# The first two tiles' modulation and the sums of the first squares on TensorE, and a longer stated landing time of loads in a list schedule

## The chip, the cores and the metric

The program runs on one core of a Trainium2 chip. The metric is the device time of one execution in microseconds (us). The kernel is written in Bass: each engine (PE is TensorE, DVE is VectorE, ACT is ScalarE, POOL is GpSimd, SP is SyncE, which issues all the DMAs here) works through its own queue in the order in which the program issued the instructions, and semaphores keep the engines in step.

## What is computed

A trunk of two layers over x (1024 tokens, 1024 channels, float32). Each sub-layer starts with an RMS norm and an adaLN modulation from a conditioning vector c. Layer 0 mixes tokens by a gated MLP, layer 1 by a gated linear recurrence; each is followed by a convolutional FFN. Cut to what matters:

```python
cond = jax.nn.silu(c)
for i in range(DEPTH):
    mod = (cond @ ada_w[i] + ada_b[i])[:, None, :]
    sh1, sc1, g1, sh2, sc2, g2 = jnp.split(mod, 6, axis=-1)
    h = rms_norm(x, norm_g[i, 0]) * (1.0 + sc1) + sh1
    y = (spatial_gating_mixer if i % 2 == 0 else hgrn2_mixer)(h, ...)
    x = x + g1 * y
    h = rms_norm(x, norm_g[i, 1]) * (1.0 + sc2) + sh2
    x = x + g2 * conv_ffn(h, ...)
return rms_norm(x, final_g)
```

The first thing that the first matrix product (h @ w_in of the mixer) needs is h: the sum of squares of x over the channels, and for each channel sc1 and sh1, two dot products of cond with columns of ada_w.

## The kernel before

x is kept transposed: eight tiles d = 0..7 of 128 channels by 1024 tokens, in two halves of 512 tokens (LO and HI). Each large product is made of float32 operands that are split into a rounded part (hi, by ACT, L500 for weights, L487 for h) and the rest (lo, by DVE or POOL, L503 and L488), and takes three matrix products for one (`mm3`, L280): hi x hi, hi x lo, lo x hi. Strassen-like combinations save products in the later stages.

**What sets the order.** All work is entered in a plan (`pl.op`) with the engine, a stated duration, what it reads and writes, and a priority. `Plan.schedule` is a list schedule over the stated durations: it takes again and again the operation that can start earliest, by priority where several can. A result of a DMA counts as there LOAD = 2.0 us after the stated end of its transfer (`lag`); loads that `p_ada` enters count ADA_LAG = 1.5 us later still. The schedule is run twice; in the second run the priorities are the latest start times that follow from the PE order of the first. The instructions are then issued in that order, so a stated time moves instructions in every queue, but no instruction waits for a stated time.

**The start.** The program's first work is this:
- PE multiplies a tile of ones by itself as a filler (`warm`, L968), 14 times, later 10 and 8 times; nothing reads the result.
- SP issues the loads of x (LO) in five transfers (L996), the row of c behind the third of them (L994), then rows of ada_w (two 512 KB transfers a tile, one for the scale and one for the shift), parameters and weights of the values (wv), in the order A0 W W A1 W A2 W ... W W W W of the loop over items.
- PE broadcasts the row of c to all partitions by two products with ones (L1004); ACT and DVE make silu of it (L1006, L1007).
- ACT squares the eight tiles of x (L454, the last by L1016), DVE adds the first seven squares into one tile (L459), and PE sums the last square and that tile over the partitions: eight products with a column of ones (L1020).
- DVE makes the inverse root of the four columns (L314 to L324) and spreads it into a diagonal (L368), PE broadcasts that by a product with ones (L373).
- For each tile d, `first_values` makes the two dot products of cond with rows of ada_w on DVE (L288, a multiply over 128 x 1024 with its sum), adds the bias (L296), makes the factor (L300), and multiplies x by it and the inverse root (L1042); ACT and DVE make the hi and lo part of h from it (L487, L488). For tile 0 one of the dot products is entered ahead (`p_dot`).
- `first_mms` enters the products of tile d with the split weights: eight PSUM banks, three products each. For tile 0 the eight hi x hi products come first by themselves.

After these come the rest of the values, the spatial gating (`GmUp`), the output product (`block_out`, read out by L442 of `p_evac`), the FFN (`Ffn`), the recurrence (`HgUp`, `Unit`), and the second FFN. The dot products for the later modulations are entered through all these stages by `p_ada`, one transfer and one DVE instruction each.

## Time and profile before

| | before |
|---|---|
| median of 3 runs | 2400.89 us |
| lowest and highest | 2396.86 and 2404.48 us |
| the profiled execution | 2402.39 us |
| its span, from the first to the last instruction | 2400.6 us |
| mean granted clock of PE in it | 0.994 |
| PE busy | 2370.1 us (99% of the span) |
| DVE busy | 2063.9 us (86%) |
| ACT busy | 1288.8 us (54%) |
| POOL busy | 449.9 us (19%) |

The profile is of one execution. Times are counted from its first instruction. A float32 product stands in it as two records, one that came from rounded operands as one. PEclk is the share of the full TensorE clock (2.4 GHz) that was granted; 0.50 is the lower of its two levels, 1.2 GHz. A busy PE is not a PE at its peak.

### The profile page before, as it was taken

To read this page: it belongs to the slowest core of one execution; us is meant where nothing else is said; L and a number is where in the kernel's file an instruction comes from. 1 tells how busy PE (TensorE), PEld (TensorE's weight loads), DVE (VectorE), ACT (ScalarE), POOL (GpSimd) and SP (SyncE) were. 2 spreads that over 40 slices of the span, in tenths; PEclk is the share of its full clock that TensorE was granted. 3 is DMA by queue.
4 is the path that set the end of the run, shared out by engine and by line. 5 is a ranking of instruction groups with operands and counts; after the bars stand their busy time and mean duration, and the time that the engine had idled before them with its cause. 6 is when DMAs were issued, how large, how long until landed. Compare 5 with 4: busy or idle time off the path is not lost.

```text
span 2400.6 us, 32858 instructions
## 1 busy us (share of the span) xinstructions
PE 2370.1 (99%) x11358; PEld 1976.7 (82%) x11358; DVE 2063.9 (86%) x3322; ACT 1288.8 (54%) x2301; POOL 449.9 (19%) x312
## 2 busy tenths in 40 slices
PE   9999999999999999999999999999999999999998
PEld 7888887788888888888788888888888888887886
DVE  8899988988989889998988788887689988898756
ACT  4546664455555555445566666665255555544444
POOL 0222110322222221012301111111122222220121
PEclk8999999999999999999999999999999999999999
DMA  9667769720333324865301111225313333338332
GB/s 338 194 217 255 238 205 308 258 81 27 123 96 121 113 92 143 296 218 180 122 15 52 45 45 45 71 62 157 105 42 110 104 117 108 107 123 285 95 104 97
DMA packets 154827, 330.91 MB, mean 138 GB/s; under 512 B 15522, under 2 KB 34338, under 8 KB 154660
## 3 DMA queue, kind: packets, MB, share of 16 engines
q1 hardware_dynamic: 154660, 328.81, 41.8%
q8 instruction: 89, 1.46, 0.3%
q14 instruction: 78, 0.64, 0.1%
HBM read 253.77 MB, written 74.98 MB: 137 GB/s over the span
## 4 chain that ended last, share of the span: by engine, by line
PE 93%; DVE 2%; DMA 2%; issue 1%; ACT 1%; POOL 0%; SPq 0%; POOLq 0%; ACTq 0%; DVEq 0%
PE pb L280 85%; PE pb L1626 4%; PE pb L1346 1%; PE pb L1691 1%; PE pb L1711 1%; DMA h<-act 0%; PE pb L1713 0%; DVE w L503 0%; DMA xT<-vd 0%; PE pb L373 0%; DVE h L503 0%; PE pb L1684 0%; PE pb L1734 0%; DMA h<-gact 0%; DMA w<-in_down 0%
## 5 line engine op out<-in xcount | busy, mean ns | idle before, releaser
L280 PE MATMUL pb<-h,w 128*128 128x512 f32 (+1 forms) x4470 | 1038.5, 388 | 8.5 <-ACT h L500 2.9
L280 PEld LDWEIGHTS pb<-h,w 128*128 128x128 f32 x4470 | 832.5, 188 | 184.8 <-ACT h L500 4.2
L280 PE MATMUL pb<-n,w 128*128 128x512 f32 x3312 | 790.1, 391 | 1.8 <-ACT wk L735 1.0
L280 PEld LDWEIGHTS pb<-n,w 128*128 128x128 f32 x3312 | 617.6, 188 | 130.7 <-ACT wk L735 1.5
L503 POOL TENSOR_TENSOR w<-w,w 128x512 fp32r<-128x512 f32 x170 | 260.5, 1537 | 952.2 <-ACT w L500 913.9
L500 ACT ACTIVATE w<-w 128x512 fp32r<-128x512 f32 x405 | 249.8, 627 | 265.4 <-PE pb L280 162.0
L893 DVE SCALAR_TENSOR_TENSOR raw<-wk,prm,raw 128x1024 f32<-128x1024 f32 x168 | 266.3, 1594 | 7.4 <-ACT raw L889 6.3
L503 DVE TENSOR_TENSOR w<-w,w 128x512 fp32r<-128x512 f32 x235 | 169.8, 728 | 32.6 <-ACT w L500 31.7
L500 ACT ACTIVATE w<-n 128x512 fp32r<-128x512 f32 x136 | 85.8, 631 | 163.8 <-PE pb L280 151.6
L735 ACT ACTIVATE wk<-pb 128x512 f32<-128x512 f32 x160 | 94.7, 593 | 139.9 <-PE pb L280 117.7
L280 PE MATMUL pb<-w,n 128*128 128x512 f32 x612 | 144.5, 397 | 3.6 <-DVE n L488 3.6
L738 DVE TENSOR_TENSOR wk<-pb,wk 128x512 f32<-128x512 f32 x160 | 108.3, 686 | 45.5 <-PE pb L280 40.8
L280 PEld LDWEIGHTS pb<-w,n 128*128 128x128 f32 x612 | 116.5, 191 | 29.8 <-DVE n L488 4.5
L503 POOL TENSOR_TENSOR w<-raw,w 128x512 fp32r<-128x512 f32 x55 | 78.5, 1440 | 328.6 <-ACT w L500 216.9
L503 DVE TENSOR_TENSOR w<-n,w 128x512 fp32r<-128x512 f32 x136 | 101.1, 746 | 44.5 <-ACT w L500 44.1
L500 ACT ACTIVATE h<-h 128x512 fp32r<-128x512 f32 x198 | 121.8, 618 | 25.1 <-DMA h<-gact 12.8
L889 ACT ACTIVATE raw<-wk,prm 128x1024 f32<-128x1024 f32 x84 | 103.6, 1240 | 32.8 <-DVE raw L510 12.9
L280 PE MATMUL pb<-w,h 128*128 128x512 f32 x480 | 116.9, 396 | 0.0
L503 DVE TENSOR_TENSOR h<-h,h 128x512 fp32r<-128x512 f32 x150 | 110.2, 739 | 6.9 <-ACT h L500 6.9
L503 POOL TENSOR_TENSOR h<-h,h 128x512 fp32r<-128x512 f32 x48 | 67.9, 1414 | 197.9 <-ACT h L500 186.2
L280 PEld LDWEIGHTS pb<-w,h 128*128 128x128 f32 x480 | 88.1, 188 | 17.4
L442 DVE SCALAR_TENSOR_TENSOR xT<-pb,mod,xT 128x512 f32<-128x512 f32 (+1 forms) x108 | 74.4, 727 | 24.5 <-PE pb L280 24.2
(278 smaller groups left out, 2927.9 us busy)
## 6 DMA issues: line engine op xcount, KB each, us to landing
w<-in_up SPq DMA_DIRECT2D x88, 512.0 KB, 3.7
act<-raw SPq DMA_DIRECT2D x154, 256.0 KB, 2.2
h<-act SPq DMA_DIRECT2D x124, 256.0 KB, 2.8
h<-in_ada SPq DMA_DIRECT2D x45, 512.0 KB, 4.7
wk<-in_ada SPq DMA_DIRECT2D x33, 512.0 KB, 4.6
n<-in_down SPq DMA_DIRECT2D x64, 256.0 KB, 5.4
gact<-xT SPq DMA_DIRECT2D x56, 256.0 KB, 3.8
h<-gact SPq DMA_DIRECT2D x56, 256.0 KB, 3.9
```

What stands on the lines that cost most here:

```text
L280: PE.matmul(ps, L[i // 2], R[i % 2], start=first and i == 0 and not more, stop=last and i == 2, skip_group_check=more)
L442: V.scalar_tensor_tensor(out=xT[:, d, hs], in0=ps.f, scalar=gate(d), in1=xT[:, d, hs], op0=ALU.mult, op1=ALU.add)
L500: pl.op("S", 0.2 + 0.43 * w, lambda: S.activation(hi.r, src.f, AF.Copy), r=(src,), w=(hi,), pr=pr)
L503: lambda: e.tensor_tensor(out=lo.r, in0=src.f, in1=hi.f, op=ALU.subtract), *preds,
L735: pl.op("S", 0.6, lambda: S.activation(c.f, ps.f, AF.Copy), r=(ps,), w=(c,), pr=p(i) - 10)
L738: pl.op("V", 0.69, lambda: V.tensor_tensor(out=c.f, in0=ps.f, in1=c.f, op=ALU.add), r=(ps, c), w=(c,), pr=p(i) - 8)
L889: pl.op("S", 1.22, lambda: S.activation(y.f, wk[:, o + PADW:o + PADW + T], AF.Identity, bias=pc("conv_b", l * NUP + b), scale=cw(2)), r=(c ...
L893: pl.op("V", 1.26, lambda w=w: V.scalar_tensor_tensor(out=y.f, in0=wk[:, o + w:o + w + T], scalar=cw(w), in1=y.f, op0=ALU.mult, op1=ALU.ad ...
L1346: PE.matmul(ps.f[:, i * P:(i + 1) * P], v.f[:, i * P:(i + 1) * P], wsT[:, j, :], start=True, stop=True)
L1626: PE.matmul(ps_()[0:m, c, :], K.f[:, c * P:c * P + m], q, start=True, stop=True)
L1691: PE.matmul(b2.f[:, cs(c)], kT.f[:, cs(c)], vc(c), start=True, stop=True)
L1711: PE.matmul(b3.f[:, cs(c)], sc.f[:, cs(c)], vc(c), start=True, stop=s_ is None)
```

## The change

Three things change.
- **Sums of squares.** ACT squares all eight tiles into four buffers in turn (L1028 of the changed kernel), and PE sums each square by four products with a column of ones as it comes (L1032): 32 products that add up in one bank. DVE adds no squares.
- **Modulation of tiles 0 and 1.** c is loaded a second time as columns (`cc`, 128 x 8), ACT and DVE make silu of it, and for tiles 0 and 1 PE makes the two dot products each with the weights laid out in another way in memory (`adaf`): eight products with one column each (`pe_dots`, L1051). `first_values` reads the sums from PSUM. Tiles 2 to 7 keep DVE's dot products.
- **The stated times.** LOAD is 3.0 and ADA_LAG 0.5. Fillers are 7, 4 and 4; in the plan a second group of them has 3 rather than 10, all into another bank.

The two loads of c now stand ahead of x in SP's queue. The split of the first weights no longer has the first tile ahead of it in the plan.

```diff
-ADA_LAG = 1.5
+ADA_LAG = 0.5
+NPE = 2
-    LOAD = 2.0
+    LOAD = 3.0
...
-    def ada_group(l, w, d=0, n=KT, nw=1):
+    def ada_group(l, w, d=0, n=KT, nw=1, ps=None):
...
-        V.tensor_tensor(out=v, in0=v, in1=cols(pc("ada_b", l * 48, 48)), op=ALU.add)
+        src = v if ps is None else ps.rearrange("p (w d) -> p w d", d=n)
+        V.tensor_tensor(out=v, in0=src, in1=cols(pc("ada_b", l * 48, 48)), op=ALU.add)
...
-    pl.op("D", 0.1, lambda: nc.sync.dma_start(condr[0:1, :], a["crow"]), w=(rv(2),), pr=SB - 31)
+    def load_cond():
+        nc.sync.dma_start(cc, a["ccol"])
+        nc.sync.dma_start(condr[0:1, :], a["crow"])
+    pl.op("D", 0.2, load_cond, w=(ccrg, rv(2)), pr=SB - 32)
+    pl.op("S", 0.25, lambda: S.activation(csig, cc, AF.Sigmoid), w=(ccrg,), pr=SB - 32)
+    pl.op("V", 0.17, lambda: V.tensor_tensor(out=csl, in0=cc, in1=csig, op=ALU.mult), w=(ccrg,), pr=SB - 32)
...
-    warm(10, 0.3, SB - 29)
+    warm(3, 0.3, SB - 29)
...
-    for d in range(KT - 1):
-        p_sum(pl, nm0, d, accv, sqs3, SB - 3)
-    pl.op("S", 0.63, lambda: S.activation(sq.f, xT[:, KT - 1, LO], AF.Square), r=(xrg(KT - 1, LO),), w=(sq,), pr=SB - 3)
-    for i, x in enumerate((sq, accv)):
+    for d in range(KT):
+        q = sqs.next()
+        pl.op("S", 0.6, lambda d=d, q=q: S.activation(q.f, xT[:, d, LO], AF.Square), r=(xrg(d, LO),), w=(q,), pr=SB - 25 + d)
...
+                PE.matmul(ps0.f[:, c:c + 1], q.f[:, c * P:(c + 1) * P], ones[:, 0:1], start=d == 0 and c == 0,
+                          stop=d == KT - 1, skip_group_check=True)
+        last = pl.op("PE", 0.7, fn, r=(q, onesrg), w=(ps0,), pr=SB - 25 + d)
+    warm(4, 0.22, SB - 40, last)
...
+    def pe_dots(d, raws):
+
+        for m, raw in raws:
+            def fn(raw=raw, col=m // KT):
+                for k in range(KT):
+                    PE.matmul(psd[d].f[:, col:col + 1], raw.f[:, k * P:k * P + P], csl[:, k:k + 1], start=k == 0, stop=k == KT - 1)
+            pl.op("PE", 1.2, fn, r=(raw, ccrg), w=(psd[d],), pr=SB - 2.5 + d)
...
-            ada_group(0, 0, d, 1, 2)
+            ada_group(0, 0, d, 1, 2, psd[d].f[:, 0:2] if d < NPE else None)
...
-            p_load(pl, x, a["ada"][0, m], pr)
-        if d == 0:
-            p_dot(*raws.pop(0), SB, after)
+            p_load(pl, x, a["adaf"][m // KT, d] if d < NPE else a["ada"][0, m], pr)
+        if d < NPE:
+            pe_dots(d, raws)
+            raws = []
```

PE's queue from the program's first instruction to the first L280 product, before (pb6 holds the sums, h6 and the like are weight buffers):

```order
L968 MATMUL pb7_82<-ones_69 128x128 x14
L1004 MATMUL pb4_79<-raw2_67,ones_69 128x512
L1004 MATMUL pb5_80<-raw2_67,ones_69 128x512
L1020 MATMUL pb6_81<-ones_69,wk_68 128x1 x8
L968 MATMUL pb7_82<-ones_69 128x128 x10
L373 MATMUL pb6_81<-wk_68,ones_69 128x512
L968 MATMUL pb7_82<-ones_69 128x128 x8
L280 MATMUL pb0_75<-w4_177,n000_203 128x512
```

The same stretch of PE's queue in the changed kernel, whose lines are one to thirty higher (L281 is L280 of before, L375 is L373, L970 is L968):

```order
L970 MATMUL pb3_78<-ones_69 128x128 x7
L1015 MATMUL pb4_79<-raw2_67,ones_69 128x512
L1015 MATMUL pb5_80<-raw2_67,ones_69 128x512
L1032 MATMUL pb6_81<-ones_69,wk_68 128x1 x32
L970 MATMUL pb3_78<-ones_69 128x128 x4
L1051 MATMUL pb7_82<-cc_74,h6_114 128x1 x8
L1051 MATMUL pb7_82<-cc_74,h7_129 128x1 x8
L375 MATMUL pb6_81<-wk_68,ones_69 128x512
L970 MATMUL pb3_78<-ones_69 128x128 x4
L1051 MATMUL pb5_80<-cc_74,h11_141 128x1 x8
L1051 MATMUL pb5_80<-cc_74,h0_189 128x1 x8
L281 MATMUL pb0_75<-w4_211,n000_225 128x512
```

The sums have grown from 8 to 32 products, tile 0's dot products stand between them and the broadcast, tile 1's between the broadcast and the first L281 product.

DVE's queue from the diagonal of the inverse root to the low part of tile 0, before:

```order
L368 TENSOR_TENSOR wk<-prm,small 128x512
L288 SCALAR_TENSOR_TENSOR h_119,mod<-h_119,raw_67 128x1024
L288 SCALAR_TENSOR_TENSOR h_128,mod<-h_128,raw_67 128x1024
L296 TENSOR_TENSOR mod<-mod,prm 128x2
L300 SCALAR_TENSOR_TENSOR amul<-mod,prm 128x1
L1042 SCALAR_TENSOR_TENSOR xT<-xT,amul,pb_81 128x512
L503 TENSOR_TENSOR w_200<-h_135,w_167 128x1024
L503 TENSOR_TENSOR w_205<-h_143,w_177 128x1024
L288 SCALAR_TENSOR_TENSOR h_163,mod<-h_163,raw_67 128x1024
L288 SCALAR_TENSOR_TENSOR h_173,mod<-h_173,raw_67 128x1024
L296 TENSOR_TENSOR mod<-mod,prm 128x2
```

The same stretch of DVE's queue in the changed kernel (L370, L1062, L505 and L490 are L368, L1042, L503 and L488 of before):

```order
L370 TENSOR_TENSOR wk<-prm,small 128x512
L298 TENSOR_TENSOR mod<-pb_82,prm 128x2
L302 SCALAR_TENSOR_TENSOR amul<-mod,prm 128x1
L1062 SCALAR_TENSOR_TENSOR xT<-xT,amul,pb_81 128x512
L505 TENSOR_TENSOR w_223<-h_158,w_201 128x1024
L505 TENSOR_TENSOR w_238<-h_165,w_211 128x1024
L298 TENSOR_TENSOR mod<-pb_80,prm 128x2
L302 SCALAR_TENSOR_TENSOR amul<-mod,prm 128x1
L1062 SCALAR_TENSOR_TENSOR xT<-xT,amul,h_236 128x512
L490 SCALAR_TENSOR_TENSOR n_241<-xT,mod,n_225 128x512
L505 TENSOR_TENSOR w_260<-h_199,w_243 128x1024
L490 SCALAR_TENSOR_TENSOR n_267<-xT,mod,n_256 128x512
```

The four dot products are gone from it, and the two groups wait for PE's sums in PSUM (pb_82 and pb_80) instead.

DVE's queue in the output product of layer 0, between the read-out of banks 6 and 7 (pb_81, pb_82) and that of bank 0 (pb_75), before:

```order
L442 SCALAR_TENSOR_TENSOR xT<-pb_82,mod,xT 128x512
L503 TENSOR_TENSOR w_2897<-raw_65,w_2897 128x512
L503 TENSOR_TENSOR h_3019<-h_2967,h_3019 128x512
L503 TENSOR_TENSOR w_2937<-raw_65,w_2937 128x512
L503 TENSOR_TENSOR h_3035<-h_2962,h_3035 128x512
L288 SCALAR_TENSOR_TENSOR h_3209,mod<-h_3209,raw_67 128x1024
L503 TENSOR_TENSOR w_2826<-n_2842,w_2826 128x512
L296 TENSOR_TENSOR mod<-mod,prm 128x8
L300 SCALAR_TENSOR_TENSOR amul<-mod,prm 128x8
L288 SCALAR_TENSOR_TENSOR raw_66,mod<-raw_66,raw_67 128x1024
L503 TENSOR_TENSOR w_2855<-n_2848,w_2855 128x512
```

The same place of DVE's queue in the changed kernel (L444 is L442 of before, L289 is L288):

```order
L289 SCALAR_TENSOR_TENSOR h_3234,mod<-h_3234,raw_67 128x1024
L505 TENSOR_TENSOR w_2934<-raw_65,w_2934 128x512
L505 TENSOR_TENSOR h_3076<-h_3004,h_3076 128x512
L444 SCALAR_TENSOR_TENSOR xT<-pb_81,mod,xT 128x512
L444 SCALAR_TENSOR_TENSOR xT<-pb_82,mod,xT 128x512
L505 TENSOR_TENSOR w_2974<-raw_65,w_2974 128x512
L505 TENSOR_TENSOR h_3080<-h_2999,h_3080 128x512
L298 TENSOR_TENSOR mod<-mod,prm 128x8
L302 SCALAR_TENSOR_TENSOR amul<-mod,prm 128x8
L505 TENSOR_TENSOR w_2861<-n_2878,w_2861 128x512
L289 SCALAR_TENSOR_TENSOR h_3234,mod<-h_3234,raw_67 128x1024
L505 TENSOR_TENSOR w_2891<-n_2884,w_2891 128x512
```

One dot product and two splits that stood behind the read-out of banks 6 and 7 stand ahead of it now.

## Rows read from the trace of the kernel before

**Rows 1.** The page, busy us (share of the span) xinstructions of each engine.

```profile
PE 2370.1 (99%) x11358; PEld 1976.7 (82%) x11358; DVE 2063.9 (86%) x3322; ACT 1288.8 (54%) x2301; POOL 449.9 (19%) x312
```

**Rows 2.** Windows, the dense stretch: us, busy by engine, PEclk, DMA share, GB/s.

```profile
26.55:2388.30 2361.75, 2348.01 (x11262) 1958.91 (x11262) 2041.08 (x3268) 1274.56 (x2283) 446.19 (x303) 1.00 0.42 135
```

**Rows 3.** Timeline, PE's first 50 us: start, us, line, tiles, records, idle before.

```profile
1.05 5.29 PE L968 MATMUL pb<-ones 128*128 128x128 f32 x28 [1.05 <-DVE ones L992]
7.28 2.64 PE L1004 MATMUL pb<-raw,ones 1*128 1x512 f32 x4 [0.94 <-DMA raw<-in_crow]
9.86 3.57 PE L1020 MATMUL pb<-ones,wk 128*128 128x1 f32 x16
13.29 4.61 PE L968 MATMUL pb<-ones 128*128 128x128 f32 x20
17.70 1.53 PE L373 MATMUL pb<-wk,ones 128*128 128x512 f32 x2
19.06 1.95 PE L968 MATMUL pb<-ones 128*128 128x128 f32 x16
20.82 2.10 PE L280 MATMUL pb<-w,n 128*128 128x512 f32 x8
26.55 23.63 PE L280 MATMUL pb<-w,n 128*128 128x512 f32 x91 [3.62 <-DVE n L488]
```

**Rows 4.** Timeline, DVE's first 28 us.

```profile
13.47 0.16 DVE L314 TENSOR_SCALAR small<-pb 128x4 f32<-128x4 f32 x1 [0.50 <-PE pb L1020]
...
15.45 0.69 DVE L368 TENSOR_TENSOR wk<-prm,small 128x512 f32<-128x512 f32 x1
...
19.27 0.75 DVE L1042 SCALAR_TENSOR_TENSOR xT<-xT,amul,pb 128x512 f32<-128x512 f32 x1 [0.45 <-PE pb L373]
19.93 2.35 DVE L503 TENSOR_TENSOR w<-h,w 128x1024 fp32r<-128x1024 f32 x2
22.20 1.22 DVE L288 SCALAR_TENSOR_TENSOR h<-h,raw 128x1024 f32<-128x1024 f32 x1
...
25.75 0.75 DVE L488 SCALAR_TENSOR_TENSOR n<-xT,mod,n 128x512 fp32r<-128x512 f32 x1
```

**Rows 5.** Windows, stretches of one clock level in the first 60 us.

```profile
5.05:8.47 3.42, 2.48 (x14) 1.76 (x14) 2.16 (x4) 2.95 (x6) 0.00 (x0) 1.00 1.05 401
8.47:13.20 4.73, 4.73 (x18) 3.34 (x16) 3.28 (x5) 3.79 (x7) 0.00 (x0) 0.50 1.03 406
13.20:18.70 5.50, 5.50 (x24) 4.98 (x24) 4.82 (x17) 2.49 (x3) 0.00 (x0) 0.50 1.02 408
...
25.53:32.36 6.83, 5.81 (x14) 4.56 (x15) 6.73 (x12) 3.10 (x4) 0.00 (x0) 0.50 1.01 340
...
40.00:60.00 20.00, 20.00 (x90) 16.53 (x90) 19.32 (x36) 9.10 (x13) 0.00 (x0) 1.00 0.85 307
```

**Rows 6.** Groups by form, PE, near 82 us: busy us, mean ns, idle.

```profile
L363 PE MATMUL pb<-ones,wk 128*128 128x1 f32 x8 | 0.9, 239 | 0.0
```

**Rows 7.** Timeline, SP's queue, the first issues.

```profile
0.74 1.47 SPq L996 DMA_DIRECT2D xT<-in_x  x3
2.24 0.37 SPq L994 DMA_DIRECT2D raw<-in_crow  x1
```

**Rows 8.** Timeline, ACT's squares and sigmoids in the first 14 us.

```profile
4.78 1.15 ACT L454 ACTIVATE wk<-xT 128x512 f32<-128x512 f32 x2 [2.77 <-DMA xT<-in_x]
...
9.12 0.61 ACT L454 ACTIVATE wk<-xT 128x512 f32<-128x512 f32 x1
...
11.05 1.08 ACT L1006 ACTIVATE xT<-pb 128x512 f32<-128x512 f32 x2
```

**Rows 9.** Waits of PE: us in total, times, longest us.

```profile
PE pb L280 <- DVE xT L442: 2.6, 1, 2.6
```

**Rows 10.** Timeline, DVE and PE at the read-out near 449 us.

```profile
446.99 1.22 DVE L288 SCALAR_TENSOR_TENSOR raw<-raw,raw 128x1024 f32<-128x1024 f32 x1
...
449.34 2.72 DVE L442 SCALAR_TENSOR_TENSOR xT<-pb,mod,xT 128x512 f32<-128x512 f32 x4
...
450.23 2.09 PE L280 MATMUL pb<-h,w 128*128 128x512 f32 x8 [2.62 <-DVE xT L442]
```

34 lines of the change are left out of this document (18 added, 16 removed).

## Prediction

> **What bounds the kernel now.** I read the page's busy times first: TensorE (PE) is busy in 99% of the span, the next engine in 86% [rows 1]. Then the busy time of one long stretch: from 26.55 to 2388.30 us PE is busy 2348.01 of 2361.75 us, so only 13.74 us of idling are spread over all that lies between the start and the tail [rows 2]. Two things follow. Whatever reaches the end must pass through PE, and a delay of PE before 26.55 has almost nothing behind it that could swallow it. So the question is when the dense stream of L280 products begins; the timeline of PE shows that at 26.55 us only eight of them have been done, at 20.82 [rows 3].
>
> What sets 26.55 now: the sums of squares end on PE at 13.43 (9.86 + 3.57); VectorE (DVE) makes the ten small steps and the diagonal, 13.47 to 16.14; PE broadcasts, 17.70 to 19.23; DVE forms tile 0 at 19.27, makes two splits, two dot products for tile 1 from 22.20 on, tile 1's group and the low part at 25.75 to 26.50 [rows 3, 4]. So the last part is DVE's, the first is PE's.
>
> A third view is needed: the granted clock. It is 0.50, the lower level of 1.2 GHz, from 8.47 to 18.70 and again from 25.53 to 32.36, else 1.00 [rows 5]. The first of these stretches matters most. It began while PE was on the condition row's products (L1004), and it stayed low although PE was busy without a gap: 4.73 of 4.73 us up to 13.20, nearly all of it on L1004 and on the one-column products L1020, then 5.50 of 5.50 on fillers (L968) and the broadcast. The clock rose only at the end of the fillers.
>
> **What the change does to PE's queue.** The order has, before the first L280 product: 7 fillers, the two condition products, 32 one-column sums, 4 fillers, 16 one-column dot products of tile 0, the broadcast, 4 fillers, 16 of tile 1. Before it was 14, 2, 8, 10, broadcast, 8. One-column products go from 8 to 64, fillers from 32 to 15.
>
> Price of a one-column product at the low clock: L1020's eight products are sixteen records in 3.57 us; without the last one's own 0.35 that is 0.215 a record, 0.43 a product. At the high clock L363's eight records of the same shape took 0.9, with a last one of about 0.24: 0.09 to 0.11 a record, 0.22 a product at the most [rows 3, 6]. So the price doubles with the low clock. The planner states 0.7 for four and 1.2 for eight, less than either.
>
> The Trainium skill ("TensorE: Matmul & The Clock Gate", Part 2, LDWEIGHTS) prices a weight load by its columns at a fixed 1.2 per ns, 107 ns for 128, whatever the array's clock. By that figure 64 records of sums would be an estimated 6.8 us at any clock; the trace disagrees at the low level with its 215 ns, and the measured price is used.
>
> I take the low clock for the whole start, because the nearest rows are L1020's own, and reason on the other case below. Then, in the time of the profiled execution:
>
> 1. Seven fillers at 0.46 (ten took 4.61) from 1.05: to 4.3. The condition row is now issued second, ahead of the x tiles, not behind three of them, so it should be there by then; its two products took 2.64, partly at the high clock [rows 3, 7]: to between 6.9 and 7.8, I take 7.2.
> 2. The x loads are issued two places later, some 0.9 us (three issues took 1.47), so the first square, at 4.78 before, comes at about 5.7 and is done at 6.3 [rows 7, 8]. A square is 0.58, its four sums 1.7, so PE sets the pace. 32 x 0.43 = 13.8: to 21.0, where it was 13.43.
> 3. Four fillers 1.8 (22.8), tile 0's sixteen dot products 6.9 (29.7), broadcast 1.53 to 1.9 (31.4). DVE's chain of 2.7 lies beside it and is ready at 23.7. Tile 0 is formed at 31.5; before at 19.27.
> 4. Four fillers (33.2), tile 1's sixteen 6.9 (40.1), eight L280 products at 0.43: to 43.5. Beside them DVE makes the two splits (2.35, after tile 0) and, after 40.1, the group (two small steps, about 0.2 each as in the chain), tile 1 and the low part (0.75 each), with gaps 2.1: ready at 42.2, before PE asks at 43.5. The saved dot products of tile 1, 2.3 us of DVE on the path before, therefore give nothing, nor do the seven additions of squares and the two of tile 0.
> 5. The clock. After 26.55 it stayed low for 5.81 us of dense products. I take the same from 40.1, to 45.9: 13.5 products at 0.43 are then done, where at 32.36 it had been 13.5 and the eight earlier ones. Delay: 45.9 - 32.36 = 13.5, and eight products at 0.22 (90 in 20.00 at the high clock [rows 5]) 1.8: 15.3 us.
>
> ScalarE's squares need the buffers that the sums free, and its second sigmoid stands behind five squares; both are done near 15, six us before anything asks. The dot products hold their four weight buffers until 40, and SyncE's queue waits there in order, with the loads of tiles 3 and 4 behind. DVE comes to tile 3 only after the low part at 42.2, a split (1.2), another low part (0.7), tile 2's two dot products (2.4), its group and forming (1.1) and a split (1.2), so near 49; loads issued between 27 and 30, when tile 0's buffers come free, have 19 us to land. Cost nothing; without that cover each us that a load is late would be a us of delay.
>
> **The stated landing time.** 2.0 becomes 3.0 for all loads, and the ada loads of the later stages keep 3.5 (2.0 + 1.5, now 3.0 + 0.5). No work is added; the order on all engines shifts. Bounds: the gain is at most the 13.74 us of rows 2; the loss has no row, and I bound it by as much again. The one large wait shows what a shift does: PE waits 2.62 us for the results read out by L442 at 447.6 to 450.2, and DVE reaches L442 at 449.34 behind two dot products of 1.22 and splits [rows 9, 10]. In the new order one of these dot products and two splits stand ahead of the read-out of pb6 and pb7 instead: 2.6 us less here, and as much more for those. I take 0, with 4 us to either side, as the largest single wait is 2.6.
>
> **Sum.** 2402.39 (the profiled execution, span 2400.6) + 15.3 + 0 = 2417.7. The median of the runs is 1.5 lower: **2416**.
>
> **The rivals.** (a) *The clock rises.* If it were high over the sums, one-column products would cost 0.22. The last square would end near 11.5 (the last took 9.12 to 9.73; 0.9 for the two issues and two sigmoids of 0.54 come before it now), the sums at 12.4, fillers 0.9, dot products 3.6 (16.9), broadcast (18.2), fillers 1.0, dot products 3.6 (22.8), eight products 1.8 (24.6). DVE's low part for tile 0 would be ready at 24.9. Dense from 24.9, not 26.55, gains 1.7, and the low stretch of 5.81 at half speed is gone, 2.9 more: 4.6 faster, at the median 2396. This is the case on the other side: not slower. It decides if the clock is high by about 8 us and stays there. For it speaks that 28 records of fillers were followed by a stretch at 1.00; against it that the clock fell during L1004 and did not come back in the 3.57 us of L1020. The Trainium skill (the same page, Part 1) says that sustained activity releases the throttle and advises keeping the engine busy; taken by itself that rule gives this rival; the trace agrees where the fillers and the dense products ran, not where L1020 did.
>
> (b) *The clock is high in part*, say from the dot products on: they save 32 x 0.21 = 6.7, fillers and broadcast 1.5, the low stretch of the dense stream 2.9, of the 15.3: 4 slower, 2405.
>
> (c) *The new order gives back more than it may*: most of the 13.74 vanishes beside the delay of the main case, 15.3 - 11: 2405. That needs all dozen waits, of several kinds, to improve together.
>
> (d) *The order costs*: new waits of 8 us beside the delay: 2424.
>
> **How the numbers follow.** Main case 0.72 (2411 to 2421: 4 us for the order, 1 for the condition row and the end of the low stretch), (a) 0.10, (b) 0.09, (c) 0.05, (d) 0.04. The range 2404 to 2422 takes in the main case, (b) and (c). A measurement of this kernel tells 0.3%, 7.2 us, from no change: slower is above 2408. The main case is slower but for a tail of some 0.02, and with (d) that makes 0.74; same is 0.22, from that tail, (b), (c) and 0.06 of (a); faster 0.04, the part of (a) in which the order gives 3 us as well.
>
> **What would show it.** In the new trace the 64 records of L1032 should stand 0.21 apart, end near 21, and the clock should read 0.50 from before them until some us after the first L281 product; tile 0 (L1062) near 31, the first L281 near 40. If the records stand 0.11 apart, rival (a) holds and step 2 fails. If PE waits between L1032's groups, squares or x loads set the pace and the step on the loads is wrong. If DVE's low part comes after the eight products, step 4 is. If the start is as worked out but the total is not, the order in the rest is the cause, and PE's idle time after the start, 13.74 now, will show it.

## The result and the profile after

| | before | after |
|---|---|---|
| median | 2402.01 us (6 runs) | 2414.31 us (6 runs) |
| lowest and highest | 2396.86 and 2404.48 us | 2411.70 and 2420.87 us |
| the profiled execution | 2402.39 us | 2420.87 us |
| its span | 2400.6 us | 2418.8 us |

The changed kernel takes 1.0057 times as long, with an interval of 1.0046 to 1.0069: 12.3 us more by the medians, 13.7 by the ratio (11 to 17 by its interval), nearly twice the 0.3% that a measurement of this kernel can tell from no change. The forecast was 2416. The profiled execution of the changed kernel is the longest of its six; that matters where its trace is summed up.

The page of the changed kernel, busy us (share of the span) xinstructions, the line that answers to [rows 1]:

```profile
PE 2393.9 (99%) x11436; PEld 1999.0 (83%) x11436; DVE 2047.3 (85%) x3309; ACT 1289.8 (53%) x2301; POOL 454.2 (19%) x312
```

PE is 23.8 us busier, and DVE 16.6 us less. The timeline of PE tells where (start, us, line, tiles, records, idle before), against [rows 3]; here L970 is the filler, L1015 the condition row's products, L1032 the sums, L1051 the dot products, L375 the broadcast and L281 the dense products:

```profile
1.05 3.36 PE L970 MATMUL pb<-ones 128*128 128x128 f32 x14 [1.05 <-DVE ones L994]
4.34 3.78 PE L1015 MATMUL pb<-raw,ones 1*128 1x512 f32 x4
8.04 13.81 PE L1032 MATMUL pb<-ones,wk 128*128 128x1 f32 x64
21.72 2.05 PE L970 MATMUL pb<-ones 128*128 128x128 f32 x8
23.57 6.83 PE L1051 MATMUL pb<-cc,h 128*128 128x1 f32 x32
30.25 2.05 PE L375 MATMUL pb<-wk,ones 128*128 128x512 f32 x2
32.10 1.91 PE L970 MATMUL pb<-ones 128*128 128x128 f32 x8
33.81 6.83 PE L1051 MATMUL pb<-cc,h 128*128 128x1 f32 x32
40.49 21.75 PE L281 MATMUL pb<-w,n 128*128 128x512 f32 x83
```

Before the first dense product PE has no gap behind 1.05 us, so the start is all PE's own work. The two loops of one-column products are the two long rows: 13.81 us for 64 records of sums (0.216 each) and twice 6.83 us for 32 of dot products (0.213 each).

DVE's timeline, against [rows 4] (L316 is the first small step, L370 the diagonal, L298 the group, L1062 the forming of a tile, L505 splits, L490 the low part):

```profile
21.89 0.16 DVE L316 TENSOR_SCALAR small<-pb 128x4 f32<-128x4 f32 x1 [6.65 <-PE pb L1032]
...
23.87 0.69 DVE L370 TENSOR_TENSOR wk<-prm,small 128x512 f32<-128x512 f32 x1
...
30.43 0.16 DVE L298 TENSOR_TENSOR mod<-pb,prm 128x2 f32<-128x2 f32 x1 [5.86 <-PE pb L1051]
...
32.34 0.75 DVE L1062 SCALAR_TENSOR_TENSOR xT<-xT,amul,pb 128x512 f32<-128x512 f32 x1 [1.56 <-PE pb L375]
33.01 2.35 DVE L505 TENSOR_TENSOR w<-h,w 128x1024 fp32r<-128x1024 f32 x2
...
41.81 0.74 DVE L490 SCALAR_TENSOR_TENSOR n<-xT,mod,n 128x512 fp32r<-128x512 f32 x1
```

Before, DVE was the last on this path; now it waits 6.65 and 5.86 us for PE. The work that was taken off DVE had become its waiting time.

The windows of the changed kernel (us, PE busy, PEld, DVE, ACT, POOL, granted clock, DMA share, GB/s), first of the end of the start, then of the whole dense stretch, then of two short stretches far behind:

```profile
40.50:46.20 5.70, 5.70 (x15) 4.44 (x16) 5.38 (x9) 2.62 (x3) 0.00 (x0) 1.00 0.64 205
46.20:60.00 13.80, 13.80 (x62) 11.44 (x61) 13.49 (x25) 5.08 (x6) 0.00 (x0) 1.00 0.87 275
...
50.00:2406.60 2356.60, 2343.72 (x11242) 1955.23 (x11240) 2025.59 (x3258) 1274.34 (x2279) 450.49 (x303) 1.00 0.41 134
...
988.30:991.60 3.30, 3.30 (x10) 2.55 (x9) 3.21 (x5) 1.14 (x3) 0.00 (x0) 0.50 0.97 313
...
2193.20:2196.50 3.30, 3.30 (x9) 2.61 (x8) 3.30 (x4) 0.07 (x1) 0.00 (x0) 0.50 1.02 363
```

The clock column has a trap. This trace holds no entry of the clock ahead of a rise at 46.18 us, so the first row prints 1.00. But its 15 dense records in 5.70 us are 0.38 apart, against 62 in 13.80 us, 0.22, in the next row: up to 46.18 us the lower level of 1.2 GHz was granted. The Trainium skill ("TensorE: Matmul & The Clock Gate", Part 1) warns that clock events in a trace can be unreliable; here the spacing of the records decides, and a run below shows nearly the same start with its clock entered as 0.50.

The third row is [rows 2] again: PE idles 12.88 us between the start and the tail (2356.60 less 2343.72), where it was 13.74. The last two rows show something that the profile of before did not have: behind waits of PE of 2.21 us at 984.67 and of 0.36 and 1.16 us at 2190.38 the clock was at its lower level from 988.26 to 991.68 us and from 2193.17 to 2196.58. At half speed each of these costs 1.7 us, an estimate: half of its 3.41 us.

The sum of the profiled executions. The clock is up at 46.18 instead of 32.36, and eight dense products fewer are done by then: 13.8 + 1.8 = 15.6 us. Idle time behind it: 12.88 - 13.74 = -0.9. The two falls of the clock: +3.4. Together 18.1, and the spans differ by 18.2. The medians differ by 12.3 only, because the profiled execution is 6.6 us above its median, and that of before 0.4 above.

### The profile page after: what moved, and what is told of

Its sections match the earlier page's. It is cut to its first block, busy times and chain, and to the rows that moved or that the text cites. A ratio compares the mean times of both kernels' runs of the same rounds, so it can differ in the third digit from the quotient of the medians.

```text
span 2418.8 us, 33051 instructions
## 1 busy us (share of the span) xinstructions
PE 2393.9 (99%) x11436; PEld 1999.0 (83%) x11436; DVE 2047.3 (85%) x3309; ACT 1289.8 (53%) x2301; POOL 454.2 (19%) x312
## 4 chain that ended last, share of the span: by engine, by line
PE 92%; DVE 4%; issue 2%; DMA 1%; ACT 1%; POOL 0%; SPq 0%; POOLq 0%; DVEq 0%; ACTq 0%
PE pb L281 82%; PE pb L1647 4%; PE pb L1367 1%; PE pb L1032 1%; PE pb L1732 1%; PE pb L1712 1%; DVE raw L895 1%; PE pb L1051 1%; DVE w L505 1%; PE pb L1734 0%; DVE h L505 0%; PE pb L375 0%; ACT xT L1344 0%; PE pb L1705 0%; PE pb L1554 0%
## 5 line engine op out<-in xcount | busy, mean ns | idle before, releaser
L281 PE MATMUL pb<-h,w 128*128 128x512 f32 (+1 forms) x4470 | 1042.3, 390 | 9.7 <-DVE h L505 3.9
L281 PEld LDWEIGHTS pb<-h,w 128*128 128x128 f32 x4470 | 834.3, 188 | 187.1 <-DVE h L505 5.4
L281 PE MATMUL pb<-n,w 128*128 128x512 f32 x3312 | 790.3, 392 | 1.4 <-ACT wk L737 1.2
L281 PEld LDWEIGHTS pb<-n,w 128*128 128x128 f32 x3312 | 617.4, 188 | 130.8 <-ACT wk L737 2.1
L505 POOL TENSOR_TENSOR w<-w,w 128x512 fp32r<-128x512 f32 x170 | 259.6, 1532 | 885.3 <-ACT w L502 803.6
L895 DVE SCALAR_TENSOR_TENSOR raw<-wk,prm,raw 128x1024 f32<-128x1024 f32 x168 | 255.6, 1536 | 13.0 <-ACT raw L891 12.1
L505 DVE TENSOR_TENSOR w<-w,w 128x512 fp32r<-128x512 f32 x235 | 168.6, 726 | 29.7 <-ACT w L502 27.5
L505 POOL TENSOR_TENSOR w<-raw,w 128x512 fp32r<-128x512 f32 x55 | 84.0, 1539 | 336.4 <-ACT w L502 273.6
L281 PE MATMUL pb<-w,n 128*128 128x512 f32 x612 | 143.7, 396 | 0.0
L281 PEld LDWEIGHTS pb<-w,n 128*128 128x128 f32 x612 | 116.7, 191 | 25.4 <-issue 1.0
L505 DVE TENSOR_TENSOR w<-n,w 128x512 fp32r<-128x512 f32 x136 | 99.4, 732 | 44.7 <-ACT w L502 43.7
L281 PE MATMUL pb<-w,h 128*128 128x512 f32 x480 | 117.0, 396 | 0.0
L505 DVE TENSOR_TENSOR h<-h,h 128x512 fp32r<-128x512 f32 x150 | 111.1, 745 | 4.5 <-ACT h L502 4.5
L505 POOL TENSOR_TENSOR h<-h,h 128x512 fp32r<-128x512 f32 x48 | 68.5, 1427 | 206.1 <-ACT h L502 194.9
L444 DVE SCALAR_TENSOR_TENSOR xT<-pb,mod,xT 128x512 f32<-128x512 f32 (+1 forms) x108 | 74.4, 728 | 34.1 <-PE pb L281 33.9
L281 PEld LDWEIGHTS pb<-w,h 128*128 128x128 f32 x480 | 88.1, 188 | 17.8
```

The costliest lines, as they stand in the source:

```text
L281: PE.matmul(ps, L[i // 2], R[i % 2], start=first and i == 0 and not more, stop=last and i == 2, skip_group_check=more)
L444: V.scalar_tensor_tensor(out=xT[:, d, hs], in0=ps.f, scalar=gate(d), in1=xT[:, d, hs], op0=ALU.mult, op1=ALU.add)
L505: lambda: e.tensor_tensor(out=lo.r, in0=src.f, in1=hi.f, op=ALU.subtract), *preds,
L895: pl.op("V", 1.26, lambda w=w: V.scalar_tensor_tensor(out=y.f, in0=wk[:, o + w:o + w + T], scalar=cw(w), in1=y.f, op0=ALU.mult, op1=ALU.ad ...
```

## The experiments

Each was timed beside the kernel before, on the same chip as that. To compare starts, I give each kernel's *dense start*: the time at which the stream of dense products would have begun, without a gap and at the high clock. For the kernel before: first dense product behind the wait at 26.55, low clock to 32.36, so half of 5.8 lost, and eight products of 0.22 done ahead: 26.55 + 2.9 - 1.8 = 27.7. For the changed kernel: 40.49, low to 46.18: 43.3.

| kernel | dense start, us | PE idle from 50 us to the tail | later falls of the clock in its profile | median, us | ratio to before |
|---|---|---|---|---|---|
| before | 27.7 | 13.74 | 0 | 2401.6 to 2402.3 | 1 |
| the change | 43.3 | 12.88 | 2 | 2414.31 | 1.0057 [1.0046, 1.0069] |
| its start alone | 42.8 | 17.56 | 0 | 2419.13 | 1.0067 [1.0055, 1.0079] |
| its stated times alone | 26.9 | 12.82 | 1 | 2399.79 | 0.9991 [0.9982, 1.0000] |
| sums and dots 128 columns wide | 27.0 | 11.70 | 2 | 2402.22 | 0.9997 [0.9988, 1.0005] |
| only the sums wide | 31.0 | 11.72 | 1 | 2407.34 | 1.0023 [1.0014, 1.0032] |
| only the sums on PE | 29.2 | 12.89 | 1 | 2405.86 | 1.0020 [1.0011, 1.0029] |
| only the dots on PE | 30.5 | 12.05 | 2 | 2405.49 | 1.0013 [1.0005, 1.0022] |
| the change with ten fillers | 43.0 | 11.23 | 2 | 2418.78 | 1.0072 [1.0059, 1.0086] |
| both wide, start rearranged | 24.9 | 10.86 | 1 | 2403.25 | 1.0003 [0.9994, 1.0012] |
| the same, times 2.0 and 1.5 | 25.5 | 11.71 | 0 | 2401.59 | 0.9998 [0.9987, 1.0009] |
| the same, times 3.0 and 1.5 | 26.2 | 11.02 | 0 | 2399.26 | 0.9985 [0.9975, 0.9994] |
| the same, times 2.5 and 0.5 | 26.8 | 14.39 | 1 | 2409.50 | 1.0022 [1.0009, 1.0034] |

The columns account for the profiles: the span of each, less its dense start, its idle time and 1.7 us for each fall, leaves 2357.8 to 2360.1 us in all thirteen. What a median differs by beside that is the spread between executions.

**The start and the stated times.** The start of the changed kernel under the old stated times:

```diff
-ADA_LAG = 0.5
+ADA_LAG = 1.5
-    LOAD = 3.0
+    LOAD = 2.0
```

> The changed start with the old stated times (2.0 and 1.5). Theory (the start costs its own delay, the order of the rest next to nothing): first L281 product near 40.5 us as in the changed kernel, low clock until about 46, and about 15.6 us slower than before, near 2417. Rival (the new order gives part of the delay back, since the changed kernel's median is only 12.3 above): the same start, and 18 us or more slower, near 2420.

Measured: 2419.13 us (2415.30 to 2422.38), 17.2 above before, between the theory's 15.6 and the rival's 18. Its first dense product in the timeline, the whole dense stretch in its windows, and its wait for the read-out in the output product of layer 0, which was [rows 9] before:

```profile
40.49 9.70 PE L281 MATMUL pb<-w,n 128*128 128x512 f32 x32
```

```profile
50.00:2408.30 2358.30, 2340.74 (x11239) 1952.28 (x11237) 2029.86 (x3258) 1271.94 (x2279) 449.58 (x303) 1.00 0.41 134
```

```profile
PE pb L281 <- DVE xT L444: 2.9, 1, 2.9
```

In the changed kernel the same row of the waits reads:

```profile
PE pb L281 <- DVE xT L444: 1.4, 1, 1.4
```

The start carries the loss. What it also does is change the idle time far behind it: 17.56 us, 3.8 more than before, under the same stated times. The new stated times take 4.7 of that away again; the wait at the read-out gives 1.5 of them. In the medians that is 4.8 us, but the two ratios' intervals overlap, so the size is not certain from the times alone.

The other half, the stated times alone in the kernel before:

```diff
-ADA_LAG = 1.5
+ADA_LAG = 0.5
-    LOAD = 2.0
+    LOAD = 3.0
```

> The kernel before with the new stated times (3.0 and 0.5) alone. Theory: start as before (first of the dense stream near 26.5), total within 2 us of before, 2400 to 2404, as waits of PE after the start change by about 1 us in sum. Rival (the order gives back some 3 us or more): 2399 or less. Other rival (the order adds waits that make the clock fall in the middle): 2404 to 2407.

Measured: 2399.79 us (2395.53 to 2404.70), 2.2 less than before, at the edge of what can be told apart and just below the theory's range. Its dense stream in the timeline, then windows of it:

```profile
25.70 24.60 PE L280 MATMUL pb<-w,n 128*128 128x512 f32 x95 [3.62 <-DVE n L488]
```

```profile
31.60:2387.70 2356.10, 2343.28 (x11250) 1955.41 (x11248) 2027.65 (x3259) 1274.28 (x2281) 447.05 (x303) 1.00 0.41 135
```

It idles 12.82 us instead of 13.74. So the stated times are worth one to five us in either start, never the loss.

**Is it the number of products, or the clock they run at?** Same products, same order, same count, but the moving operand of each sum and dot product is 128 equal columns instead of one. Nothing is taken away, and the results are read from one of the columns.

```diff
-  PE.matmul(ps0.f[:, c:c + 1], q.f[:, c * P:(c + 1) * P], ones[:, 0:1], ...
+  PE.matmul(ps0.f[:, c * P:(c + 1) * P], q.f[:, c * P:(c + 1) * P], ones, ...
...
-  PE.matmul(psd[d].f[:, col:col + 1], raw.f[:, k * P:k * P + P], csl[:, k:k + 1], ...
+  PE.matmul(psd[d].f[:, col * P:col * P + P], raw.f[:, k * P:k * P + P], csl[:, k:k + 1].to_broadcast([P, P]), ...
```

> The changed kernel, in which each one-column product of the start (sums and dot products, L1032 and L1051) has 128 equal columns instead; their number and order stay. Theory (the cost is the low clock, which these products do not end): a record keeps its 0.215 at the low level, but the clock rises 4 to 6 us after the sums begin at 8, so near 13; sums end near 17.5 instead of 21.9, first L281 near 27.5 instead of 40.5, at 1.00; 12 to 13 us faster than the changed kernel, near 2402. Rival (it is the number of products and the clock stays low whatever they are): no change against the changed kernel, 2414.

Measured: 2402.22 us (2399.15 to 2405.47). PE's timeline and two windows of it:

```profile
8.04 9.46 PE L1032 MATMUL pb<-ones,wk 128*128 128x128 f32 x64
...
18.23 3.74 PE L1051 MATMUL pb<-cc,h 128*128 128x128 f32 x32
...
27.04 23.18 PE L281 MATMUL pb<-w,n 128*128 128x512 f32 x99
```

```profile
8.05:12.35 4.30, 4.30 (x21) 4.30 (x21) 0.00 (x0) 1.08 (x3) 0.00 (x0) 1.00 1.05 406
12.40:17.30 4.90, 4.90 (x46) 4.90 (x45) 0.69 (x1) 3.25 (x6) 0.00 (x0) 1.00 1.03 410
```

The sums start at 8.04 us, as in the changed kernel. 21 records come in 4.30 us, then 46 in 4.90: the clock rises at 12.36, and from there on a record takes 0.11 us. The dots take 3.74 a tile instead of 6.83, and the dense products begin at 27.04, not 40.49, at the high clock. This is what the theory said. With 128 times the columns the loss is gone. At the low level a record costs nearly the same with one column as with 128 (0.216 and 0.213 above, 0.205 here), and at the high level too, as the run with only the sums wide shows below (0.10 to 0.11 with one column, 0.107 here), so it is not the products' own price. The difference, 16.3 us in the dense start and 12.1 in the medians, is the clock that PE did not get.

**Would more fillers have done?** The number of fillers ahead of the sums as before the change, all else as in the change.

```diff
-    warm(3, 0.3, SB - 29)
+    warm(10, 0.3, SB - 29)
```

> The changed kernel with ten fillers instead of three ahead of the sums, as before the change (nine of the fourteen in all stand ahead of the condition row's products, five behind them); sums and dots keep their one column. Theory (the fillers get the clock up near 4 to 5 us, but one-column products, 64 records of sums and 64 of dots, do not keep it): the first sums run 0.11 us a record, the clock is lost among them, the rest and the dots run at 0.21 us a record, the first trunk product starts at 34 to 41 and the clock is back 3 to 6 us behind it: 2408 to 2416. Rival (the change lost only because it started the sums with too few fillers; a clock that is up stays up on a TensorE that is never idle): sums in 7.2 us, dots 3.7 a tile, first trunk product at 25 to 27 and 2400 to 2403.

Measured: 2418.78 us (2415.96 to 2420.84). This trace holds the clock of the start, in its windows:

```profile
4.70:8.00 3.30, 3.30 (x17) 1.93 (x17) 0.69 (x1) 2.46 (x5) 0.00 (x0) 1.00 1.05 400
8.10:21.60 13.50, 13.50 (x66) 13.50 (x65) 0.69 (x1) 6.17 (x9) 0.00 (x0) 0.50 1.03 407
...
40.40:45.60 5.20, 5.20 (x13) 4.10 (x14) 4.88 (x9) 2.62 (x3) 0.00 (x0) 0.50 0.50 148
45.70:51.00 5.30, 5.30 (x25) 4.36 (x24) 5.20 (x10) 1.68 (x2) 0.00 (x0) 1.00 0.87 277
```

The fillers do get the clock up, at 4.67 us. It falls at 8.08, as the sums begin, and is back at 45.63, 5.2 us into the dense products, though PE had no gap in between. The rival is refuted. My theory had the fall somewhere among the sums, and the median is 2.8 us above its range. The fall came right at their head, behind the condition row's products and the last fillers, so this run shows only that the clock does not come back, not what takes it away.

**Each half of the new work alone.** Dots of tiles 0 and 1 back on DVE, sums on PE (a first version of this kernel gave no time):

```diff
-            ada_group(0, 0, d, 1, 2, psd[d].f[:, 0:2] if d < NPE else None)
+            ada_group(0, 0, d, 1, 2, None)
...
-        if d < NPE:
-            pe_dots(d, raws)
-            raws = []
```

> The changed kernel with tile 0's and tile 1's dots put back on VectorE (two of 1.22 us each per tile, as before the change); the 32 one-column sums on TensorE, the fillers, the stated landing time and the input of the condition's columns stay. Theory (each one-column product of the start costs 0.43 us at the low clock, and the clock stays low until the trunk's products have run): here half of the sums stand ahead of the condition row's two products, so the sums take 6.3 + 13.7 + 3.8 = up to about 24; chain and diagonal 26.6, tile 0 formed near 31.4, first trunk product near 32, the clock up some 5.8 us behind it. That is 5 to 6 us behind the 26.55 of the kernel before, less 2 to 5 us that the other stated landing time gives back: 2402 to 2406. Rival (the sums carry the whole loss and the dots cost little): first trunk product near 38 to 40 and 2411 to 2416.

Measured: 2405.86 us (2403.25 to 2410.82), 4.3 above before. Timeline of PE, then windows:

```profile
5.45 4.96 PE L1032 MATMUL pb<-ones,wk 128*128 128x1 f32 x32 [1.04 <-ACT wk L1028]
...
29.23 14.82 PE L281 MATMUL pb<-w,n 128*128 128x512 f32 x64 [1.66 <-ACT n L489]
```

```profile
7.80:20.80 13.00, 13.00 (x49) 10.44 (x48) 1.55 (x3) 7.76 (x11) 0.00 (x0) 0.50 1.03 408
20.90:28.10 7.20, 5.82 (x19) 4.20 (x19) 6.50 (x19) 0.00 (x0) 0.00 (x0) 0.50 0.30 99
28.20:34.00 5.80, 4.77 (x21) 3.96 (x22) 5.62 (x11) 2.35 (x4) 0.00 (x0) 1.00 0.83 291
```

The time is in the range expected, but not by the way expected: some 20 of the sums' 64 records ran at the high clock before it fell at 7.71, and it came back at 28.19, ahead of the first dense product, when PE had run eight records of fillers, the broadcast and eight more of fillers.

The sums put back as they were (DVE adds the squares, the old numbers of fillers), the dots on PE:

```diff
-    for d in range(KT):
-        q = sqs.next()
-        ...
+    for d in range(KT - 1):
+        p_sum(pl, nm0, d, accv, sqs3, SB - 3)
+    ...
+    warm(10, 0.22, SB - 40, last)
```

> The changed kernel with the first squares' sums put back as they were (VectorE adds seven squares, TensorE sums the two that are left with 8 one-column products, the old numbers of fillers); the 64 records of dots of tiles 0 and 1 stay on TensorE, and so does the stated landing time. Theory: tile 0's dots stand between the two halves of the sums and cost 6.8 us at the low clock, half of tile 1's dots and ten fillers stand ahead of the broadcast and half of them behind: first trunk product near 36 (34 to 38), the clock up near 42, 9 to 10 us behind the kernel before, less 2 to 5 us for the order: 2404 to 2410. Rival (the dots lie beside the squares and cost little, the sums are the loss): first trunk product at 27 to 29 and 2398 to 2403.

Measured: 2405.49 us (2402.31 to 2408.72), 3.9 above before; the ratio, which goes by all runs, says 1.2 to 5.3. Timeline of PE, then windows:

```profile
11.21 6.96 PE L1051 MATMUL pb<-cc,h 128*128 128x1 f32 x32
...
19.75 4.62 PE L970 MATMUL pb<-ones 128*128 128x128 f32 x20
24.15 2.02 PE L1051 MATMUL pb<-cc,h 128*128 128x1 f32 x16
...
30.46 15.79 PE L281 MATMUL pb<-w,n 128*128 128x512 f32 x67
```

```profile
19.80:24.50 4.70, 4.70 (x24) 4.70 (x23) 3.70 (x14) 0.07 (x1) 0.00 (x0) 0.50 0.99 390
24.60:30.40 5.80, 5.80 (x48) 5.32 (x48) 1.88 (x2) 1.21 (x2) 0.00 (x0) 1.00 0.06 16
```

Tile 0's dots run at the low clock and cost what the theory says, but the twenty records of fillers behind them bring the clock back at 24.51, and tile 1's dots then take 2.02 for sixteen records. First dense product 30.46, not 36: my expectation of the place missed by 5.5 us, the time is inside its range.

These two runs change the account. Both have the new stated times, so the run to hold them against is that of the stated times alone (dense start 26.9, median 2399.79). Against it the sums alone move the dense start by 2.3 us and the dots alone by 3.6; both together, in the changed kernel, by 16.4. In the dense start the halves don't add. In the medians they cost 6.1 and 5.7 against 14.5 for both, and those 2.7 us over the sum are too few to count. With either alone the clock returned among fillers and broadcast, at 28.19 and 24.51 us, before the dense products; the run with the dots alone also has the 32 fillers of before, not the 15 of the change. With both, PE goes from 13.8 us of sums over eight records of fillers to 6.8 us of dots, and again, and the clock returned only behind the first dense products.

**Does the clock hold over one-column products once it is up?** Only the sums 128 columns wide (the first two lines of the diff above), the dots with one column:

> The changed kernel with only its 32 sums 128 equal columns wide; the dots of tiles 0 and 1 have one column as in the change. The sums end near 17.4 and the clock is up near 12.4, as with both wide. Theory (one-column products do not keep the clock up, as those of L1020 did not in the kernel before): the clock is lost again while the 64 records of dots run, they take 0.43 us a pair from there on (up to 6.8 us a tile instead of 3.7), the first trunk product starts at 30 to 34 and comes at the low clock at first: 2405 to 2410. Rival (once the clock is up, a TensorE that is never idle keeps it whatever the products' width): dots 3.7 us a tile, first trunk product near 27, and 2402 as with both wide.

Measured: 2407.34 us (2402.70 to 2409.60). Windows, and the first dense product in the timeline:

```profile
18.80:22.30 3.50, 3.50 (x35) 3.50 (x33) 1.73 (x8) 0.00 (x0) 0.00 (x0) 1.00 1.04 382
24.10:27.10 3.00, 3.00 (x30) 3.00 (x28) 2.34 (x3) 2.15 (x3) 0.00 (x0) 1.00 0.45 158
27.20:33.90 6.70, 6.70 (x19) 5.44 (x20) 5.58 (x9) 2.62 (x3) 0.00 (x0) 0.50 0.91 334
```

```profile
28.00 18.25 PE L281 MATMUL pb<-w,n 128*128 128x512 f32 x67
```

It holds over tile 0's dots (one record per 0.10 us) and is lost at 27.17, when 30 records of tile 1's had run, with no wait of PE anywhere near. The dense products then start at the low clock and stay there to 34.00. The direction was as expected; the fall came later and the dots cost less than I had said. In this run nothing but one-column products stands in the 3.0 us ahead of the fall.

**Toward a better kernel.** Both wide, and the clock up from the first sum on: ten fillers ahead of the sums, the condition row's two products behind the broadcast (only tile 2's dots on DVE need them), and stated times of 0.9 and 1.85 us for four sums and eight dots.

```diff
-    warm(3, 0.3, SB - 29)
+    warm(10, 0.3, SB - 29)
...
     last = pl.op("PE", 0.86, lambda: nm0.bcast(ps0.f), r=(accv,), w=(ps0,), pr=SB - 3)
+    for i in range(2):
+        ...
+        pl.op("PE", 0.9, lambda c=c, b=b: PE.matmul(b.f, ones[0:1, :], c.f[0:1, :], ...), last, r=(c, onesrg),
+              w=(b,), pr=SB - 2.6)
```

> The kernel with sums and dots 128 equal columns wide, and besides: ten fillers instead of three ahead of the sums, the condition row's two 512-wide products behind the broadcast instead of ahead of the sums (only tile 2's dots on VectorE need them), and stated times of 0.9 us for four sums and 1.85 us for eight dots. Theory (the start is TensorE's path: what is run there at the high clock and what is moved off it comes back one to one): sums end at 10.5 to 11.5, diagonal near 13.5, tile 0 formed near 17, first trunk product near 18 at the high clock, tile 1's dots (3.7 us) behind some of tile 0's products; against the 27.04 of the kernel with both wide that is 5 us less after the dots: 2395 to 2399. Rival (beyond the start VectorE and the loads set the pace, 11.1 us a pair of tiles on VectorE against 10.6 on TensorE, so that what is won turns into waits between 20 and 60 us): 2400 to 2403.

Measured: 2403.25 us (2398.62 to 2405.18), ratio 1.0003 [0.9994, 1.0012]. Timeline of PE:

```profile
5.77 7.31 PE L1024 MATMUL pb<-ones,wk 128*128 128x128 f32 x64
...
21.14 2.81 PE L281 MATMUL pb<-w,n 128*128 128x512 f32 x11
...
27.28 18.90 PE L281 MATMUL pb<-w,n 128*128 128x512 f32 x81
```

The clock is up at 4.20 us, and the first dense product comes at 21.14; with eleven of them done, the dense start is 24.9, 2.8 before the kernel before. My expectation of 18 had the sums done at 10.5 to 11.5; 64 records of 0.114 are 7.3 us, and they ended at 13.1. By the median the theory (2395 to 2399) missed, and the rival's number is the nearer; but the waits that it put between 20 and 60 us are not there: PE idles 10.86 us from 27.3 us on and the same from 50 us on. The profiled execution shows the gain (2398.62), and it is the lowest of eleven: the others are 1.3 to 6.6 us longer. Its clock fell once, behind a wait of 2.03 us at 963.71. The same place of two kernels' windows, this one and the one below with stated times of 3.0 and 1.5, which had a wait of 2.21 us there:

```profile
966.80:970.10 3.30, 3.30 (x9) 2.62 (x8) 3.08 (x4) 1.09 (x3) 0.00 (x0) 0.50 1.02 336
```

```profile
967.40:970.80 3.40, 3.40 (x15) 2.83 (x16) 3.40 (x5) 1.85 (x4) 0.00 (x0) 1.00 1.04 341
```

Nearly the same wait is followed by a low clock in one execution and not in the other. So such falls may be part of the spread of the times. The mean granted clock, which is on record for every execution, points that way: it is 0.997 for the two shortest of this kernel's eleven (2398.62 and 2399.90 us) and 0.996 for the nine others. Where in those nine it was low is not shown.

Three more pairs of stated times, with the start of the last kernel:

```diff
-ADA_LAG = 0.5
+ADA_LAG = 1.5
-    LOAD = 3.0
+    LOAD = 2.0
```

> The last kernel (sums and dots 128 equal columns wide, ten fillers, condition row behind the broadcast) with the stated landing time and the lag of the kernel before (2.0 and 1.5 instead of 3.0 and 0.5). Theory (the order by 3.0 and 0.5 leaves waits of 2.0 to 2.3 us on TensorE near 200 and 965 us, after which the clock falls for 3.4 us in some executions, 1.7 us each; the order by 2.0 and 1.5 had no such wait there, and its profile from the change's start showed no fall in mid-span): no fall at 960 to 1000, granted clock 0.997 or 0.998 in most executions; waits some 4 to 5 us more, falls 2 to 5 us less: 2400 to 2405. Rival (the falls carry nothing, and the order's 4.8 us come back whole, as between the change and its start alone): 2407 to 2409.

Measured: 2401.59 us (2396.94 to 2406.61), ratio 0.9998 [0.9987, 1.0009]. No fall of the clock in mid-span, as expected, and the time is in the theory's range; but PE idles 11.71 us, 0.9 more than the 10.86 under 3.0 and 0.5 and not 4 to 5 more. And the spread of the runs is no smaller: 4.65 us lie between the profiled execution without a fall and the median.

```diff
-ADA_LAG = 0.5
+ADA_LAG = 1.5
```

> The kernel with the wide sums and dots and the order by 3.0 and 0.5, with the lag alone at 1.5, as before the change. Theory A (the gain of the order comes from the stated landing time; the lag moves loads of the next block's modulation alone): within 1.5 us of the kernel with 3.0 and 0.5, 2401.5 to 2405, with the wait near 965 us still there. Rival B (the lag carries the order's gain): 2405 to 2409, the wait near 200 or 450 us longer.

Measured: 2399.26 us (2395.81 to 2400.56), ratio 0.9985 [0.9975, 0.9994]. The wait near 965 us is there, as theory A said, but the time is the best of all, below either theory's range: by the medians 0.6% below the change, and 0.12% below the kernel before, too little to count by the 0.3% above though the interval leaves 1 out. Its windows show the idle time of the dense stretch, 11.01 us:

```profile
27.30:2383.80 2356.50, 2345.49 (x11273) 1957.46 (x11271) 2025.90 (x3271) 1279.04 (x2283) 447.46 (x303) 1.00 0.42 135
```

```diff
-    LOAD = 3.0
+    LOAD = 2.5
```

> The same kernel with a stated landing time of 2.5 us and the lag of 0.5. Theory (the stated time acts only by which waits the order happens to leave, each a few us in all): the sum of TensorE's waits behind the start within 3 us of the 12.7 of the kernel with 3.0, no trend between 2.0 and 3.0: 2398 to 2406. Rival (a stated time nearer to the true landing time is the better the longer it is): between the kernels with 2.0 and 3.0 in waits and in time.

Measured: 2409.50 us (2402.23 to 2413.24), ratio 1.0022 [1.0009, 1.0034], the longest of the four. Windows:

```profile
22.10:25.50 3.40, 3.40 (x12) 2.94 (x11) 1.29 (x2) 2.12 (x4) 0.00 (x0) 0.50 1.03 411
27.30:2389.60 2362.30, 2347.91 (x11275) 1959.90 (x11273) 2026.66 (x3271) 1280.52 (x2283) 454.71 (x303) 1.00 0.42 135
```

14.39 us idle, 3.5 more than under 3.0, one more fall far behind, and one at 22.09 with no wait near it: the condition row's products had run from 19.62 to 21.53. Both theories miss, the first by 3.5 us of time, the second because 2.5 does not lie between 2.0 and 3.0. Four pairs of stated times on one start give 2399.3 to 2409.5 us without a trend: ten us hang on numbers whose meaning for the time can't be read from them. Of the 10.2 us between the last two kernels the profiles explain some 6.

## Why the prediction was right, step by step

The forecast of 2416 stands beside 2414.31, by the case that was given most of the chance.

**The low clock for the whole start, from L1020's own rows** [rows 3, 5]: right, and it is the step on which all hangs. The records of L1032 stood 0.216 apart and those of L1051 0.213, where 0.215 was taken from eight products of before. The run with 128 columns shows that this choice was worth the loss: with the clock up at 12.36 us the same queue gives the time of before.

Two readings of the clock are off, and nothing in the sum hangs on them. In the kernel before it was not 1.00 ahead of 5.05 us: the trace holds no entry there, the trap above, and the 18 filler records in the 4.00 us up to 5.05 are 0.22 apart, the lower level, by which step 1 did price its fillers. And it rose at 18.71 us in the broadcast, not at the end of the fillers near 17.9.

**Steps 1 to 3** were late by less than one us, from one term. The condition row's products took 3.78 us, not 2.64, because here they ran at the low clock to their end; they were done near 8.0, just past the bound of 7.8. The sums then ended at 21.85 (21.0 forecast), the broadcast at 32.3 (31.4), and tile 0 was formed at 32.34 (31.5). PE set the pace of the sums, as said: ACT's squares waited for the buffers, not PE for squares.

**Step 4**: tile 1's dots ended at 40.6 (40.1 forecast), and DVE's low part was done at 42.55 (42.2), ahead of PE. The saved work of DVE gave nothing, as said; the rows of DVE above have its waits instead.

**Step 5**: the clock rose at 46.18 (45.9). Delay of the start: 15.6 us, 15.3 forecast.

**The stated times**: taken as 0, with 4 to either side. In the profile the idle time went from 13.74 to 12.88, which is 0.9 of gain. But the two experiments show that this is a sum of two terms that the step did not have apart: the later start itself made 3.8 us more idle time under the old stated times, and the new ones took 4.7 away. And it left out a third, the falls of the clock behind waits: 3.4 us in the profiled execution. The three came to 2.5 us together, and that they nearly cancel is luck. So is part of the nearness of 2416 to 2414.31: for the profiled execution the sum said 2417.7 and it took 2420.87, but the median of the changed kernel lies 6.6 us below that, where the sum took off 1.5. Bounds of 4 us to either side were not too wide, as ten us lie between the four pairs of stated times.

**The rivals.** (a), the clock rises, was decided by the clock as it said, but 2396 was too low for it: the kernel with the clock up at 12.36 us gave 2402.2, and those with the clock up near 4 to 7 us 2399.3 to 2409.5. Their dense start of 24.9 to 26.8 lies 1.8 to 3.7 us behind that of the rival, which is 23.1 by the measure of the table (its 24.9 less 1.8 for the eight products done ahead). For a PE that is never idle the Trainium skill ("TensorE: Matmul & The Clock Gate", Part 1: sustained activity releases the throttle) would have given this rival; the trace disagrees where PE ran one-column products, as it was busy from 1.05 to 46.18 us at the low clock. (b) had the clock high in part, from the dots on; its 2405 is near the 2405.5 to 2405.9 of the halves by themselves, but those have half of the new work, so they are no test of it. (c) and (d) were the order's, and the order moved the time by a few us in either direction, never by 8 to 11 in this start.

**What I did not see**: that the delay belongs to the two halves together. Priced by their records at the low clock, the sums' half costs 10.2 us (13.81 less the 3.57 of [rows 3]) and the dots' half 13.7; measured alone, against the stated times alone, they moved the dense start by 2.3 and 3.6 and the median by about 6 each.

## What to carry to other kernels

Where PE bounds a kernel, work moved to it from an engine that is not the bound is paid at the level of the clock that PE has then (the 128 records of sums and dots took 27.5 us at the lower level, and 16.9 with 128 columns, where the clock rose among them): read the spacing of the same records in the profile at hand before pricing them. If thin products stand in a queue for many us, try the same products with more columns, or fillers between the groups, before giving up the move. Here the columns were worth 12 us of 2414 and cost no time; with the dots alone the clock came back behind ten fillers between two groups, while ten instead of three ahead of the sums did not hold it. Numbers that only set an order are worth trying in pairs on the chip, each against several runs, since their effect was up to ten us here and none of it could be read from the numbers.
